# Gates and convolution inputs of a hybrid layer as seven-product blocks ahead of the attention, the convolution's projection behind it

## The chip, the cores and the metric

The kernel runs on one core of one Trainium2 chip. The metric is the device time of one execution in microseconds (us); the median of three runs before the change is 2365.08 us (2362.23 to 2366.52). One execution was taken with the hardware profiler: it took 2368.07 us, of which 2366.3 us lie between its first and last instruction. PE is the matmul engine (TensorE), ACT is ScalarE, DVE is VectorE, POOL is GpSimd, SP is the engine that issues most of the DMAs (SyncE).

## The reference, cut to what matters

One layer, sequence 1024, width 1024, all in fp32. The change is in the mixer between two feed-forward parts:

```python
h = modulate(rms_norm(x, g_mix[l]), sh2, sc2)
b_g, c_g, u, q, k, v, z_conv, z_attn = jnp.split(h @ w_in[l], IN_OFFSETS, axis=-1)
y_conv = (b_g * short_conv(c_g * u, conv_w[l])) @ w_conv_proj[l]
y_attn = sliding_window_attention(rope(q), rope(k), v, sinks[l]) @ w_attn_proj[l]
merged = sigmoid(z_conv) * y_conv + sigmoid(z_attn) * y_attn
x = x + gt2[:, None, :] * (merged @ w_out[l])
```

`short_conv` is a causal convolution of three taps in each channel. The attention has 16 heads in 4 groups and a window of 128. The feed-forward parts (inner width 2816) stand before and behind it.

## The kernel before

**Numbers.** Activations are held transposed, 8 tiles (`db` or `k`, 0 to 7) of 128 channels, in two halves `h` of 512 positions. A fp32 value is carried as two fp32r parts, hi and lo; a product of a 128x128 weight block and a 128x512 activation tile is three matmuls (`mm3`, L138, L140, L142: hi by hi, hi by lo, lo by hi). `split` makes the parts: ACT casts the hi part (L106), DVE, or POOL where the code says so, subtracts it for the lo part (L107). Tiles for weight parts turn in a ring of 8 (`w`), raw weights from DRAM in a ring of 4 (`wr`, loaded by `load_st`, L114), activations with their parts in rings of 28 (`t`, 128x2x512) and 16 (`x`, 128x512), scratch tiles (`q`, `u`, `s`) in short rings, PSUM in 8 banks (`ps`).

**Seven products.** The feed-forward parts compute a 2x2 block product with seven multiplications in place of eight (`gu_seven`, L392): `all_seven` forms the seven combinations of the activations once (DVE, L179 to L183), `seven_weights` forms those of each block's weights (DVE, L154 to L163, and seven splits), `product` (L195) issues the matmuls, 7 x 4 x 3 = 84 of 128x512 for a block, and DVE joins the partial results (L426, L432, L435). A block gives two output tiles in both halves. The mixer before does not use this.

**The mixer.** The down projection of the first feed-forward part ends with `down_part` for the last hidden tiles, half 0 and then half 1; behind tile 4 of half 1 the normalised input of half 0 is formed (`mix_h`, L275, L279, L290). The attention follows, 36 steps over 32 units (group, 128 positions); in step s stand `stage_c` of unit s-2 (scores, L853), `stage_b` of unit s-1 (transposes of q and k by PE, L832), `stage_a` of unit s (q, k, v: 24 matmuls of 128x384, L797 to L799), up to two pieces of the attention's projection (`proj_piece`, L950; its weight from `wap`, split into `t` tiles), `stage_e` of unit s-4 (L919, L920) and `stage_d` of unit s-3 (L896). Between a and b of one unit lies the rotary chain: DVE L807, L810, L813, then POOL L817, L818. In steps 0 to 4 an early gate is added (`early_gate`: 24 matmuls of one tile of z_attn, half 0, its weight in `t` tiles), in steps 0 to 3 also the mean square and `mix_h` of half 1, in steps 32 to 35 the same gates for half 1.

**The convolution's stage.** Behind the attention come the three other gates of z_attn, then for each pair of channel tiles (`gi`) the three inputs B, C and u (`wbcu`, 48 matmuls each with both halves), the taps (DVE L1056), and the projection of that pair (`wcp`), whose partial sums are added up in SBUF by DVE (L1085); then the eight gates of z_conv and the merge. 31 steps of the conditioning vector's products (`some_ada`, L225, each with a 512 KB load) lie in this stage, on a row that is loaded again (`crow_again`). `w_out` follows.

**Order.** PE runs in the order of the program. The rows of DVE, ACT, POOL and SP are put in order by a scheduler before the launch; each engine then works strictly in that order.

Of the kernel before, what the change touches and what calls it, by code (L numbers as in the profile page):

```python
# [13 lines left out]
P = 128  # L14
D = 1024
# [20 lines left out]
def tile_macaron_layer(  # L36
# [303 lines left out]

    class Hidden:
# [12 lines left out]
        def keep(self, t, dst):  # L354
            hi = tile_x(F32R)
            nc.scalar.copy(hi, t)  # L356
            nc.vector.tensor_tensor(f32r(t), t, f32(hi), op=ALU.subtract)  # L357
            nc.sync.dma_start(dst[:, 0, :], f32(hi))
            nc.sync.dma_start(dst[:, 1, :], t)

        def put(self, j, h, t):
            if j >= 4 * NCH:
                self.keep(t, self.last[j - 4 * NCH][h])
                return
# [9 lines left out]
            for k in PRODS:  # L374
                self.keep(parts[k], self.seven[p][k])
# [16 lines left out]
    def gu_seven(wgu, js, hid, ts, extra=lambda: None):  # L392
# [4 lines left out]
        def prep(j):  # L397
            ra, rb = load_st(wgu[j, 0]), load_st(wgu[j, 1])
            return seven_weights(ra[:, :HALF], ra[:, HALF:], rb[:, :HALF], rb[:, HALF:])

        def tail(state):

            j, w, oa, sa0 = state
            product(oa, w["q4"], xs["q4"], c0s, False, True)
            nc.vector.scalar_tensor_tensor(
                out=(raw := tile_x()), in0=oa, scalar=-1.0, in1=sa0, op0=ALU.mult, op1=ALU.mult)
            hid.put(j, 0, raw)

        ahead = [prep(j) for j in js[:1]]
        before = None  # L410
        for n, j in enumerate(js):
            w = ahead.pop(0)
            if n + 1 < len(js):
                ahead.append(prep(js[n + 1]))
# [4 lines left out]
            if before:  # L419
                tail(before)  # L420
# [5 lines left out]
            nc.vector.tensor_tensor(r1, r1, ob, op=ALU.add)  # L426
            nc.scalar.activation(r1, r1, AF.Silu)
# [7 lines left out]
            nc.vector.tensor_tensor(r5, r5, oa, op=ALU.add)  # L435
            nc.vector.scalar_tensor_tensor(
                out=(raw := tile_x()), in0=r5, scalar=-1.0, in1=r2, op0=ALU.mult, op1=ALU.mult)
            hid.put(j, 1, raw)
            extra()
            before = (j, w, oa, r1)  # L440
        tail(before)
# [151 lines left out]
    with tc.tile_pool(name="f1", bufs=2) as tmp:  # L593
# [143 lines left out]
        some_ada(6)  # L737
        gu_seven(w1gu, range(3, NJ), hid, ts, lambda: some_ada(1))
# [33 lines left out]
        hh, hl = hh2, hl2  # L772


    yat = by_half(tile_x)
# [516 lines left out]
```

## Time and profile before

| what | value |
|---|---|
| median of 3 runs | 2365.08 us |
| profiled execution | 2368.07 us, span 2366.3 us, mean granted PE clock 0.981 |
| PE busy | 2270.1 us (96%) |
| DVE busy | 1574.8 us (67%) |
| ACT busy | 1019.4 us (43%) |
| POOL busy | 395.0 us (17%) |
| read from DRAM, written | 256.19 MB, 91.49 MB |

PE is the engine to read first: its busy share is 96%, so time is lost only where PE waits or where its granted clock is below 1. The views used below are the page, groups of instructions by line (busy time, mean of one, idle time ahead and what ended it), waits, and busy time in chosen stretches. In the rows `ps<-t,w` means output from inputs; a row of the stretches gives for each engine busy time and, in brackets, the instructions.

### The profile page before, as it was taken

The page shows a single profiled execution, that of the slowest core. Times are in us where ns is not written, and L with a number is a line of the kernel's source. Part 1 is how long each engine was busy: PE and PEld are TensorE (multiplying, and loading weights), DVE is VectorE, ACT ScalarE, POOL GpSimd, SP SyncE. Part 2 cuts the span into 40 slices and gives each one's busy share as a digit, 9 for nine tenths or more (in the row PEclk, how much of TensorE's full clock was granted, in tenths as well). Part 3 has the DMA queues.
Part 4 walks back from the last instruction along what each step waited for, and adds up shares of the span by engine and source line. Part 5 has one row for each costly group of instructions (what it writes and reads, how often), then busy time and mean ns, then how long its engine had stood idle before and what let it go on. Part 6 is the DMA issues. An engine that isn't in the chain of part 4 may idle for free.

```text
span 2366.3 us, 30044 instructions
## 1 busy us (share of the span) xinstructions
PE 2270.1 (96%) x10608; PEld 1898.0 (80%) x10608; DVE 1574.8 (67%) x2796; ACT 1019.4 (43%) x2009; POOL 395.0 (17%) x461
## 2 busy tenths in 40 slices
PE   5899999999987899998999999999999999999997
PEld 4688888888876799996788888888888888888786
DVE  8888777858864567775543544444687776676875
ACT  4544444544443566554223121123554444454342
POOL 3000000006561334442000000001100000002644
PEclk9899999999998999998999999999999999999998
DMA  8165446799531201212422332115324553389922
GB/s 312 62 223 204 144 142 213 254 406 296 168 133 40 70 20 60 64 30 81 165 94 88 103 98 63 54 45 196 107 64 159 178 177 126 116 319 335 330 101 72
DMA packets 131767, 349.65 MB, mean 148 GB/s; under 512 B 18720, under 2 KB 20896, under 8 KB 131616
## 3 DMA queue, kind: packets, MB, share of 16 engines
q1 hardware_dynamic: 127008, 339.34, 40.9%
q0 software_dynamic: 4608, 8.39, 2.0%
q8 instruction: 83, 1.36, 0.2%
q14 instruction: 68, 0.56, 0.1%
HBM read 256.19 MB, written 91.49 MB: 147 GB/s over the span
## 4 chain that ended last, share of the span: by engine, by line
PE 86%; DVE 8%; DMA 2%; ACT 2%; issue 1%; POOL 0%; SPq 0%; DVEq 0%; ACTq 0%; POOLq 0%
PE ps L195 43%; PE ps L142 12%; PE ps L140 11%; PE ps L138 11%; PE ps L799 2%; PE ps L797 2%; PE ps L798 2%; DVE w L107 1%; PE ps L853 1%; DVE x L530 1%; PE ps L896 1%; DVE t L225 1%; DMA wr<-in_w2d_dram 1%; DVE u L275 1%; DMA x<-in_x_dram 1%
## 5 line engine op out<-in xcount | busy, mean ns | idle before, releaser
L195 PE MATMUL ps<-t,w 128*128 128x512 f32 x4956 | 1126.9, 390 | 5.5 <-DVE x L530 2.8
L195 PEld LDWEIGHTS ps<-t,w 128*128 128x128 f32 x4956 | 931.0, 188 | 201.0 <-DVE r L435 3.9
L106 ACT CAST w<-wr 128x512 fp32r<-128x512 f32 (+1 forms) x410 | 249.5, 612 | 637.5 <-PE ps L195 298.7
L107 DVE TENSOR_TENSOR w<-wr,w 128x512 fp32r<-128x512 f32 (+1 forms) x394 | 296.1, 756 | 213.3 <-ACT w L106 212.0
L140 PE MATMUL ps<-t,w 128*128 128x512 f32 (+1 forms) x1024 | 341.7, 388 | 4.7 <-DVE t L290 4.7
L476 POOL TENSOR_TENSOR x<-x,g 128x512 f32<-128x512 f32 x96 | 145.1, 1525 | 1061.5 <-DVE x L530 588.8
L138 PE MATMUL ps<-t,w 128*128 128x512 f32 (+1 forms) x896 | 292.7, 389 | 7.1 <-ACT t L279 7.1
L142 PE MATMUL ps<-t,w 128*128 128x512 f32 (+1 forms) x896 | 291.1, 387 | 0.0
L140 PEld LDWEIGHTS ps<-t,w 128*128 128x128 f32 x1024 | 193.8, 189 | 45.4 <-DVE t L290 6.9
L138 PEld LDWEIGHTS ps<-t,w 128*128 128x128 f32 x896 | 169.9, 190 | 43.2 <-ACT t L279 9.7
L142 PEld LDWEIGHTS ps<-t,w 128*128 128x128 f32 x896 | 169.7, 189 | 33.7
L106 ACT CAST w<-ws 128x512 fp32r<-128x512 f32 x177 | 109.7, 620 | 183.2 <-PE ps L195 137.7
L107 DVE TENSOR_TENSOR w<-ws,w 128x512 fp32r<-128x512 f32 x177 | 123.6, 704 | 31.5 <-ACT w L106 31.2
L138 PE MATMUL ps<-t,t 128*128 128x512 f32 x240 | 103.3, 431 | 25.4 <-ACT t L106 22.4
L142 PE MATMUL ps<-t,t 128*128 128x512 f32 x240 | 102.3, 426 | 5.1 <-DVE t L107 5.0
L140 PE MATMUL ps<-t,t 128*128 128x512 f32 x240 | 101.5, 423 | 0.9 <-POOL t L931 0.9
L530 DVE SCALAR_TENSOR_TENSOR x<-ps,mods,x 128x512 f32<-128x512 f32 (+1 forms) x104 | 73.0, 708 | 31.2 <-PE ps L195 15.9
L357 DVE TENSOR_TENSOR x<-x,x 128x512 fp32r<-128x512 f32 x145 | 91.9, 690 | 1.5 <-ACT x L356 1.4
L799 PE MATMUL ps<-w,t 128*128 128x384 f32 x256 | 87.7, 343 | 4.5 <-DVE t L290 4.5
L319 POOL TENSOR_TENSOR s<-s,q 128x512 f32<-128x512 f32 (+1 forms) x48 | 55.0, 1146 | 217.7 <-ACT q L315 216.1
L797 PE MATMUL ps<-w,t 128*128 128x384 f32 x256 | 89.4, 349 | 0.0
L798 PE MATMUL ps<-w,t 128*128 128x384 f32 x256 | 86.8, 339 | 0.0
(162 smaller groups left out, 2787.5 us busy)
## 6 DMA issues: line engine op xcount, KB each, us to landing
t<-hs SPq DMA_DIRECT2D x140, 512.0 KB, 9.9
hs<-x SPq DMA_DIRECT2D x277, 256.0 KB, 4.6
wr<-in_wada_dram SPq DMA_DIRECT2D x56, 512.0 KB, 3.7
wr<-in_w1gu_dram SPq DMA_DIRECT2D x44, 512.0 KB, 4.5
wr<-in_w2gu_dram SPq DMA_DIRECT2D x44, 512.0 KB, 3.6
wr<-in_wbcu_dram SPq DMA_DIRECT2D x24, 512.0 KB, 3.5
wr<-in_w1d_dram SPq DMA_DIRECT2D x22, 512.0 KB, 7.5
wr<-in_w2d_dram SPq DMA_DIRECT2D x22, 512.0 KB, 7.6
```

The lines of the kernel that those rows point to most:

```text
L106: nc.scalar.copy(hi, src)
L107: lo_engine.tensor_tensor(lo, src, f32(hi), op=ALU.subtract)
L138: mm(o, wh, xh, start=start, stop=False)
L140: mm(o, wh, xl, start=False, stop=False)
L142: mm(o, wl, xh, start=False, stop=stop)
L195: mm(o, a, b, start=first, stop=last, skip_group_check=True)
L357: nc.vector.tensor_tensor(f32r(t), t, f32(hi), op=ALU.subtract)
L476: nc.gpsimd.tensor_tensor(dst, dst, r, op=ALU.add)
L530: nc.vector.scalar_tensor_tensor(out=dst, in0=src, scalar=gate[:, db : db + 1], in1=dst if base is None else base, op0=ALU.mult, op1=ALU.add,)
L797: mm(o[:, :384], xh, wh, start=k == 0, stop=False)
L798: mm(o[:, :384], xh, wl, start=False, stop=False)
L799: mm(o[:, :384], xl, wh, start=False, stop=k == KT - 1)
```

## The change

All inputs of the mixer but q, k, v move ahead of the attention. Four gate tiles (tiles 0 and 1 of z_attn and z_conv) are plain products, 192 matmuls, written so that half 0 runs while half 1 is normalised; the mean square of half 1 stands at their k = 2, its `mix_h` at k = 4. Then `all_seven` forms the combinations and 18 blocks run as one stream: 6 pairs of gate tiles (`Gates`), 8 blocks of C and u (`Taps`, which form C times u and the convolution) and 4 of B (`Gated`, which multiply by the convolution). Sigmoids (32 tiles of 256 KB), the parts of the convolved input (`ycv`, 16 of 512 KB) and four combined tiles that are overwritten (`h12`) go to DRAM. The attention's steps carry no gates any more. The projection of the convolution (`conv_proj`, 24 matmuls with all eight input tiles summed in one bank) stands in the last attention steps and behind them; it reads `ycv` (`load_y`) and two gate tiles each. The same matmuls add up to: gates and convolution inputs 1920 before, 192 + 18 x 84 = 1704 now; the projection 384 in both. Loads of ACT's tables fall from 20 to 9, DMAs that SP issues rise from 882 to 986. The two feed-forward parts use the same code through classes; one `some_ada` step moves ahead of the first, 30 lie in the stream, up to three at a gate block and one at each other.

```diff
+    def seven_stream(blocks, ts, extra):
...
+            to.c21(oa)
...
+            to.c11(r1, ob)
...
+            to.c22(r5, oa)
+            extra(to)
+            before = (w, oa, to)
+        tail(*before)
...
+        some_ada(7)
+        gu_seven(w1gu, range(3, NJ), hid, ts, lambda to: some_ada(1))
...
+        def keep_gate(src, which, db, h, sign=1.0):
+            sg = tile_x()
+            nc.scalar.activation(sg, src, AF.Sigmoid, scale=sign)
+            nc.sync.dma_start(gates[which][db][h], sg)
+
+        class Gates(SevenOut):
+            def __init__(self, which, db):
+                self.at = (which, db)
+
+            def c11(self, r1, ob):
+                super().c11(r1, ob)
+                keep_gate(r1, *self.at, 0)
+
+            def c12(self, r2, oc):
+                super().c12(r2, oc)
+                keep_gate(r2, *self.at, 1)
+
+            def c22(self, r5, oa):
+                super().c22(r5, oa)
+                keep_gate(r5, self.at[0], self.at[1] + 1, 1, -1.0)
+
+            def c21(self, oa):
+                keep_gate(oa, self.at[0], self.at[1] + 1, 0, -1.0)
...
+                self.cu = [None, negative_product(r5, self.y12)]
+
+            def c21(self, oa):
+                self.cu[0] = negative_product(oa, self.y11)
...
+                for h in range(2):
+                    cu, t = self.cu[h], tile_x()
+                    nc.scalar.mul(t, cu, cw[2])
+                    for back in (1, 2):
+                        w = cw[2 - back]
+                        pieces = [(t[:, back:], cu[:, : HALF - back])]
+                        if h == 1:
+                            pieces.append((t[:, :back], self.cu[0][:, HALF - back :]))
+                        for dst, src in pieces:
+                            nc.vector.scalar_tensor_tensor(
+                                out=dst, in0=src, scalar=w, in1=dst, op0=ALU.mult, op1=ALU.add)
+                    convolved[self.i, h] = t
...
+            def done(self, i, h, b, sign=1.0):
+                t = convolved.pop((i, h))
+                if sign > 0:
+                    nc.vector.tensor_tensor(t, b, t, op=ALU.mult)
+                else:
+                    negative_product(b, t, t)
+                keep_parts(t, ycv[i][h])
...
+        plain = [(1, 0), (1, 1), (0, 0), (0, 1)]
+        wg = [load_w(wz[which, db]) for which, db in plain]
+
+        def some_gates(idx, h, between=lambda k: None):
+            banks = [bank() for _ in idx]
+            for k in range(KT):
+                between(k)
+                for i, o in zip(idx, banks):
+                    mm3([o], wg[i](k * P), [(hh[k][h], hl[k][h])], k == 0, k == KT - 1)
+            for i, o in zip(idx, banks):
+                keep_gate(o, *plain[i], h)
+
+        def between(k):
+            if k == 2:
+                rs[1] = stats[1].rstd()
+            if k == 4:
+                pb = spread(rs[1])
+                for d in range(KT):
+                    mix_h(pb, d, 1)
+
+        some_gates(range(4), 0, between)
+        ts = all_seven(tt, xT)
+        some_gates((0, 1), 1)
+        some_gates((2,), 1)
+        some_gates((3,), 1)
+
+        def gate_pair(which, db):
+            return wz[which, db], wz[which, db + 1], Gates(which, db)
+
+        def conv_pair(i):
+            return [(wbcu[k, 1], wbcu[k, 2], Taps(k)) for k in (i, i + 2)] + [
+                (wbcu[i, 0], wbcu[i + 2, 0], Gated(i, i + 2))]
+
+        seven_stream(
+            [gate_pair(1, 2), gate_pair(0, 2)] + conv_pair(0) + [gate_pair(1, 4)] + conv_pair(1)
+            + [gate_pair(0, 4)] + conv_pair(4) + [gate_pair(1, 6)] + conv_pair(5)
+            + [gate_pair(0, 6)],
+            ts, lambda to: some_ada(3 if isinstance(to, Gates) else 1),
+        )
...
+        for k in range(4):
+            t = tile_t()
+            nc.sync.dma_start(f32(t), h12[k])
+            hh[k][1], hl[k][1] = pair_of(t)
...
+        def load_y(h):
+            for i in range(KT):
+                t = tile_t()
+                nc.sync.dma_start(f32(t), ycv[i][h])
+                yparts[i, h] = pair_of(t)
+
+        def load_wc(dq):
+            wc[dq] = [load_w(wcp[g, dq]) for g in range(4)]
...
+        def conv_proj(db, h):
+
+            o = bank()
+            for i in range(KT):
+                c0 = (i % 2) * 512 + (db % 4) * P
+                mm3([o], wc[db // 4][i // 2](c0), [yparts[i, h]], i == 0, i == KT - 1)
+            sc, sa = stored_gate(0, db, h), stored_gate(1, db, h)
+            nc.vector.tensor_tensor(sc, sc, o, op=ALU.mult)
+            nc.vector.tensor_tensor(yat[db][h], yat[db][h], sa, op=ALU.mult)
+            nc.vector.tensor_tensor(sc, sc, yat[db][h], op=ALU.add)
             if h == 0:
+                ml[db] = tile_c(F32R)
+            mh[db][h] = tile_x(F32R)
+            split(mh[db][h], ml[db][:, h * HALF : (h + 1) * HALF], sc)
...
-            if s == 0:
-                rs[1] = stats[1].rstd()
-            if 1 <= s <= 3:
-                if s == 1:
-                    pb = spread(rs[1])
-                for d in ((0, 1, 2), (3, 4, 5), (6, 7))[s - 1]:
-                    mix_h(pb, d, 1)
-            if s >= len(units):
-                early_gate(s - len(units), 1)
+            if s == len(units):
+                load_wc(0)
+                load_y(0)
+                load_y(1)
...
-            if s < 5:
-                early_gate(s, 0)
-        early[4] = sigmoid(gate_tiles(1, 4, (1,))[0], "u")
+            if s > len(units):
+                conv_proj(s - len(units) - 1, 0)
+        conv_proj(3, 0)
+        for db in range(4):
+            conv_proj(db, 1)
+        load_wc(1)
+        for db in range(4, KT):
             for h in range(2):
-                nc.vector.tensor_tensor(yat[db][h], yat[db][h], sigmoid(o[h]), op=ALU.mult)
...
-        ycv = [tile_c(F32) for _ in range(KT)]
-        for gi in range(4):
-            ys = []
-            for i in (2 * gi, 2 * gi + 1):
...
-                for t in (1, 2, 0):
-                    w = load_w(wbcu[i, t])
...
-                        mm3(banks[t], w(k * P),
-                            [(hh[k][h], hl[k][h]) for h in range(2)], k == 0, k == KT - 1)
-                    some_ada(2 if t == 2 else 1)
...
-                        if gi == 0:
-                            nc.scalar.copy(dst, o[h])
-                        else:
-                            nc.vector.tensor_tensor(dst, dst, o[h], op=ALU.add)
...
+                conv_proj(db, h)
```

**PE, first steps of the attention.** Before, between the last matmuls of `stage_a` and the transposes of `stage_b` (L832) for the same unit stand the 24 matmuls of an early gate, of which the last three are shown; then `stage_a` of the next unit begins.

```order
L138 MATMUL ps_5991<-t_5838,t_5984 128x512
L140 MATMUL ps_5991<-t_5838,t_5984 128x512
L142 MATMUL ps_5991<-t_5838,t_5984 128x512
L832 MATMUL ps_6022<-ident,q_5960 128x128 x3
L797 MATMUL ps_6031<-w_5901,t_5803 128x384
L798 MATMUL ps_6031<-w_5901,t_5803 128x384
L799 MATMUL ps_6031<-w_5901,t_5803 128x384
```

Now the transposes (L1010) stand directly behind `stage_a` of the same unit (L975 to L977).

```order
L975 MATMUL ps_9069<-w_9064,t_5852 128x384
L976 MATMUL ps_9069<-w_9064,t_5852 128x384
L977 MATMUL ps_9069<-w_9064,t_5852 128x384
L1010 MATMUL ps_9109<-ident,q_9098 128x128 x3
L975 MATMUL ps_9118<-w_9039,t_5810 128x384
L976 MATMUL ps_9118<-w_9039,t_5810 128x384
L977 MATMUL ps_9118<-w_9039,t_5810 128x384
```

What stood between a unit's `stage_a` and its `stage_b` on PE has moved away.

**DVE, around the last feed-forward tiles.** Here `u` and `t` (L275, L290) are the normalised input of half 0. Before, the lo parts of the early gate's weight (L107, into `t` tiles) follow behind all eight, and the rotary chain of unit 0 (L807) is next.

```order
L290 SCALAR_TENSOR_TENSOR t_5823<-u_5824,mods,t_5823 128x512
L275 SCALAR_TENSOR_TENSOR u_5839<-x_3957,amod,ps_5798 128x512
L290 SCALAR_TENSOR_TENSOR t_5828<-u_5829,mods,t_5828 128x512
L290 SCALAR_TENSOR_TENSOR t_5833<-u_5834,mods,t_5833 128x512
L290 SCALAR_TENSOR_TENSOR t_5838<-u_5839,mods,t_5838 128x512
L107 TENSOR_TENSOR t_5983<-wr_5985,t_5983 128x512
L107 TENSOR_TENSOR t_5984<-wr_5985,t_5984 128x512
L807 TENSOR_TENSOR u_5958<-ps_5931,rope_5956 128x320
```

Now the lo parts of the fourth plain gate's weight go into the `w` ring, and stand among the same rows.

```order
L290 SCALAR_TENSOR_TENSOR t_5822<-u_5823,mods,t_5822 128x512
L290 SCALAR_TENSOR_TENSOR t_5828<-u_5829,mods,t_5828 128x512
L275 SCALAR_TENSOR_TENSOR u_5853<-x_3960,amod,ps_5805 128x512
L107 TENSOR_TENSOR w_5968<-wr_5966,w_5968 128x512
L290 SCALAR_TENSOR_TENSOR t_5834<-u_5835,mods,t_5834 128x512
L107 TENSOR_TENSOR w_5969<-wr_5966,w_5969 128x512
L290 SCALAR_TENSOR_TENSOR t_5840<-u_5841,mods,t_5840 128x512
L290 SCALAR_TENSOR_TENSOR t_5846<-u_5847,mods,t_5846 128x512
L290 SCALAR_TENSOR_TENSOR t_5852<-u_5853,mods,t_5852 128x512
```

The split of that weight has moved in among the L290 rows, ahead of four of them and behind the rest; the last of these rows belongs to k = 7.

**ACT, end of the attention.** The weight that is waited for is that of the attention's projection for the last group (`t` tiles from `wr`). Before, its two casts (third and fourth row) stand ahead of the four exponentials (L870) of unit 30.

```order
L106 CAST t_10199<-wr_10201 128x512
L106 CAST t_10200<-wr_10201 128x512
L106 CAST t_10234<-wr_10236 128x512
L106 CAST t_10235<-wr_10236 128x512
L106 CAST ws_10194<-ps_10190 128x256
L930 CAST t_9731<-s_10133 128x2x128
L870 ACTIVATE t_10170,den_10172<-t_10170,negm_10171 128x256 x4
L877 ACTIVATE es_10173<-es_10173 128x4
L106 CAST t_9270<-ps_10190 128x128
```

Now the cast of the same weight (last row, `t_13157`) stands behind the casts of the convolution's projection (`w`, of which the last is the first row), the copies, the exponentials (L1048) and the casts that follow them.

```order
L106 CAST w_13120<-wr_13117 128x512
L999 CAST vt_12999<-ps_12964 128x2x64
L1104 COPY s_13027<-ps_13018 64x256
L106 CAST t_13034<-ps_13036 128x512
L106 CAST t_13034<-ps_13043 128x512
L106 CAST ws_13088<-ps_13084 128x256
L1104 COPY s_13027<-ps_13018 64x256
L1048 ACTIVATE t_13064,den_13066<-t_13064,negm_13065 128x256 x4
L106 CAST t_12164<-ps_13084 128x128
L1108 CAST t_12625<-s_13027 128x2x128
L1055 ACTIVATE es_13067<-es_13067 128x4
L106 CAST t_13157<-wr_13159 128x512
```

The projection's weight has moved behind the exponentials of unit 30, on which it does not depend.

More of the change, by code (lines that the diff above doesn't have):

```diff
@@ L339, in swiglu_raw, with keep_parts @@
         return dst
+    def keep_parts(t, dst):
+        hi = tile_x(F32R)
+        nc.scalar.copy(hi, t)
+        nc.vector.tensor_tensor(f32r(t), t, f32(hi), op=ALU.subtract)
+        nc.sync.dma_start(dst[:, 0, :], f32(hi))
+        nc.sync.dma_start(dst[:, 1, :], t)
     class Hidden:
@@ L352, in __init__ @@
                          for _ in range(2)]
[L354 to L359, printed above, removed]
         def put(self, j, h, t):
             if j >= 4 * NCH:
-                self.keep(t, self.last[j - 4 * NCH][h])
+                keep_parts(t, self.last[j - 4 * NCH][h])
                 return
@@ L374, in put @@
             for k in PRODS:
-                self.keep(parts[k], self.seven[p][k])
+                keep_parts(parts[k], self.seven[p][k])
     def gu_mm(outs, w, hh, hl, halves):
@@ L399, in prep, with tail @@
             return seven_weights(ra[:, :HALF], ra[:, HALF:], rb[:, :HALF], rb[:, HALF:])
-        def tail(state):
-            j, w, oa, sa0 = state
+        def tail(w, oa, to):
             product(oa, w["q4"], xs["q4"], c0s, False, True)
[L405 to L409, printed above, removed]
+            to.c21(oa)
+        ahead = [prep(blocks[0])]
@@ L410, in gu_seven @@
         before = None
-        for n, j in enumerate(js):
+        for n, (_, _, to) in enumerate(blocks):
             w = ahead.pop(0)
-            if n + 1 < len(js):
-                ahead.append(prep(js[n + 1]))
+            if n + 1 < len(blocks):
+                ahead.append(prep(blocks[n + 1]))
             oa, oc = bank(), bank()
@@ L431, in gu_seven @@
             product(oc, w["q3"], xs["q3"], c0s, False, True)
-            nc.vector.tensor_tensor(r2, r2, oc, op=ALU.add)
-            nc.scalar.activation(r2, r2, AF.Silu)
+            to.c12(r2, oc)
             product(oa, w["q7"], xs["q7"], c0s, False, True)
[L435 to L441, printed above, removed]
+            to.c22(r5, oa)
+            extra(to)
+            before = (w, oa, to)
+        tail(*before)
+    def gu_seven(wgu, js, hid, ts, extra=lambda to: None):
+        seven_stream([(wgu[j, 0], wgu[j, 1], GateValue(hid, j)) for j in js], ts, extra)
     def down_seven(wd, hid, gate, ngate, xs, residual, extra=lambda: None):
@@ L775, in tile_macaron_layer @@
+        assert not steps
+        for k in range(4):
+            t = tile_t()
+            nc.sync.dma_start(f32(t), h12[k])
+            hh[k][1], hl[k][1] = pair_of(t)
     yat = by_half(tile_x)
```

171 lines of the change are left out of this document (71 added, 100 removed).

## The prediction

> **What bounds the kernel now.** I read the page first, then the busy time in stretches, then PE's waits, then the mean of one instruction by line.
>
> ```profile
> PE 2270.1 (96%) x10608; PEld 1898.0 (80%) x10608; DVE 1574.8 (67%) x2796; ACT 1019.4 (43%) x2009; POOL 395.0 (17%) x461
> ...
> L195 PE MATMUL ps<-t,w 128*128 128x512 f32 x4956 | 1126.9, 390 | 5.5 <-DVE x L530 2.8
> ```
>
> PE is busy in 96% of the span and DVE in 67%, so PE sets the time wherever it neither waits nor runs at a reduced clock. Where in the mixer does it do that? The stretches are the end of the down projection, the attention's start, its middle, its tail, the gates behind it, and the convolution's stage up to `w_out`. Columns: width, then busy time of PE, PEld, DVE, ACT and POOL, the granted PE clock, DMA share, GB/s.
>
> ```profile
> 672.22:698.40 26.18, 23.62 (x112) 19.54 (x111) 16.29 (x25) 13.80 (x23) 18.30 (x16) 1.00 0.49 171
> 698.40:803.00 104.60, 82.12 (x389) 67.79 (x387) 50.63 (x130) 45.69 (x103) 20.74 (x33) 0.82 0.15 49
> 803.00:1062.00 259.00, 256.81 (x1680) 235.51 (x1681) 191.73 (x610) 159.98 (x501) 110.81 (x196) 0.99 0.16 50
> 1062.00:1131.00 69.00, 57.18 (x263) 45.07 (x262) 36.12 (x72) 35.89 (x78) 13.63 (x18) 0.90 0.30 100
> 1131.00:1140.00 9.00, 9.00 (x41) 7.46 (x40) 7.91 (x13) 2.81 (x3) 0.00 (x0) 1.00 0.92 325
> 1140.00:1608.00 468.00, 468.00 (x2066) 387.66 (x2065) 210.78 (x332) 106.56 (x183) 2.17 (x15) 1.00 0.25 80
> ```
>
> Loss is width less PE's busy time, plus width times the missing part of the clock. The start loses 104.6 - 82.1 = 22.5 idle and 0.18 x 104.6 = 18.8 by the clock, **41.3**. The middle loses 2.2 + 2.6 = **4.8**, the tail 11.8 + 6.9 = **18.7**, together **64.8 us**. The convolution's stage loses nothing: 468.00 busy in 468.00 at clock 1.00. There only fewer matmuls help.
>
> ```profile
> PE ps L138 <- ACT t L106: 22.4, 8, 4.4
> PE ps L142 <- DVE t L107: 5.0, 6, 2.2
> PE ps L799 <- DVE t L290: 4.5, 5, 1.9
> PE ps L269 <- DVE nr L260: 2.6, 1, 2.6
> ```
>
> Columns: what waits and for what, us in total, times, longest. The 22.4 us are eight waits for weights of the early gates and of the attention's projection, whose casts stand behind other work on ACT.
>
> ```profile
> 724.00:728.00 4.00, 1.46 (x12) 1.27 (x10) 3.32 (x8) 1.94 (x4) 1.10 (x2) 1.00 0.06 12
> 728.00:732.00 4.00, 2.35 (x6) 1.63 (x7) 2.93 (x5) 1.39 (x3) 0.00 (x0) 0.72 0.05 7
> 732.00:736.00 4.00, 4.00 (x11) 3.13 (x10) 0.00 (x0) 0.00 (x0) 0.00 (x0) 0.50 0.31 93
> ```
>
> Behind one such wait: PE is idle most of 724 to 728, and the clock is 0.72 and then 0.50 in the next two stretches. A gap of about 4 us thus costs up to 4 x 0.28 + 4 x 0.50 = 3.1 us more.
>
> **The matmuls.** Gates and inputs fall from 1920 to 192 + 18 x 84 = 1704 matmuls of 128x512, 216 fewer.
>
> ```profile
> 672.22 0.39 PE L138 MATMUL ps<-t,w 128*128 128x512 f32 x1
> ...
> 688.09 0.39 PE L140 MATMUL ps<-t,w 128*128 128x512 f32 x1
> ```
>
> The listed 0.39 us is a pipelined length. Between these two rows lie 70 steps at full clock: 15.87 / 70 = 0.2267 us from start to start. So 216 x 0.2267 = **49.0 us** less; a block of 84 is 19.04 us of PE. The projection's 384 matmuls only move.
>
> **The stream of blocks.** Does DVE keep up with 19.04 us a block? Its durations:
>
> ```profile
> L107 DVE TENSOR_TENSOR w<-wr,w 128x512 fp32r<-128x512 f32 (+1 forms) x394 | 296.1, 756 | 213.3 <-ACT w L106 212.0
> L107 DVE TENSOR_TENSOR w<-ws,w 128x512 fp32r<-128x512 f32 x177 | 123.6, 704 | 31.5 <-ACT w L106 31.2
> L435 DVE TENSOR_TENSOR r<-r,ps 128x512 f32<-128x512 f32 x39 | 26.8, 687 | 21.4 <-PE ps L195 21.4
> L357 DVE TENSOR_TENSOR x<-x,x 128x512 fp32r<-128x512 f32 x145 | 91.9, 690 | 1.5 <-ACT x L356 1.4
> L1056 DVE SCALAR_TENSOR_TENSOR q<-ws,v,q 128x512 f32<-128x512 f32 x32 | 24.0, 750 | 1.9 <-ACT q L1054 1.8
> L225 DVE CUSTOM_DVE_ANT_0 wr<-wr,crow_again,v 128x1024 f32<-128x1024 f32 x31 | 39.8, 1285 | 63.9 <-DMA wr<-in_wada_dram 60.0 <-ACT crow_again L1028 3.9
> L275 DVE SCALAR_TENSOR_TENSOR u<-t,amod,ps 128x512 f32<-128x512 f32 x16 | 10.8, 742 | 3.9 <-PE ps L269 3.9
> L290 DVE SCALAR_TENSOR_TENSOR t<-u,mods,t 128x512 fp32r<-128x512 f32 x48 | 40.6, 873 | 1.1 <-ACT t L279 0.8
> L181 DVE SCALAR_TENSOR_TENSOR x<-x,x 128x512 f32<-128x512 f32 x28 | 19.3, 690 | 0.0
> L107 DVE TENSOR_TENSOR t<-x,t 128x512 fp32r<-128x512 f32 x32 | 20.8, 695 | 0.0
> ```
>
> A block's weights take four sums at 0.69 and seven lo parts, 4 x 0.756 + 3 x 0.704, together 7.9 us; the three joins 3 x 0.687 = 2.1. `Gates` add three conditioning steps of 1.285 (some 1.37 with the read of the sum): 14.1 in all. `Taps` add two products (1.4), four taps at 0.75, two pieces of one and two columns (some 0.4) and one conditioning step: 16.2. `Gated` add four products and four lo parts at 0.69 (5.5) and one such step: 16.9; but where the three steps of the gate block behind are put early into it, 19.6, 0.6 over PE. I take 1 us for each of the four, **+4**. Bounds: 0, and 14: the row L225 shows 60.0 us of waiting for such loads, some 2 for each of its 31, and seven of the stream's 30 such waits would reach PE in full. I cost stores (19 MB) and loads at nothing: with the blocks' and the conditioning weights some 53 MB in 343 us, 156 GB/s, beside 325 GB/s that the row 1131 to 1140 moved. Without that cover rival 3 holds.
>
> **The plain gates' start.** The normalisation of half 0 is as before; now 12 matmuls (2.7 us) stand at each k. The first lo part comes 2.7 late, about the 2.6 of row L269. The fourth weight's lo part stands among the L290 rows, four at 0.873 ahead: 3.2. The mean square 0.6, half clock 2: **+8.5** (3 to 12; the 4.5 of row L799, which is in the start's 41.3, goes).
>
> **DVE behind it.** From the spread of half 1 to the last join of the first block DVE has 8 x 0.742 + 8 x 0.873 (normalisation, 12.9), 16 combinations at 0.69 (11.0), 16 lo parts at 0.695 (11.1), 13 lo parts of weights (9.5), 8 sums (5.6), three conditioning steps (4.1) and three joins (2.1): 56.3 us. PE's work in that time: four k of four gates 10.9, half 1 of them 96 x 0.2267 = 21.8, one block 19.0, another product 2.7: 54.4. With the waits between rows **+5** (0 to 9).
>
> **The attention's start.** With the early gates their waits go; what is late next is the rotary chain, which their matmuls covered.
>
> ```profile
> L853 PE MATMUL ps<-t,ws 64*128 64x256 f32 (+1 forms) x384 | 30.9, 293 | 0.0
> L896 PE MATMUL ps<-ident,t 128*128 128x128 f32 x240 | 31.4, 273 | 0.0
> L807 DVE TENSOR_TENSOR u<-ps,rope 128x320 f32<-128x320 f32 x32 | 15.6, 489 | 8.4 <-PE ps L799 6.7 <-issue 1.6
> L813 DVE TENSOR_TENSOR q<-ps,rope 128x160 f32<-128x160 f32 x32 | 10.1, 315 | 0.0
> L817 POOL TENSOR_TENSOR q<-u,q 128x320 f32<-128x320 f32 x32 | 28.5, 891 | 65.6 <-DVE q L813 54.4 <-PE ps L142 6.6 <-DVE den L879 4.6
> L818 POOL COPY q<-q 128x64 f32<-128x64 f32 x32 | 8.6, 268 | 1.6
> ```
>
> DVE 0.489 + 2 x 0.315 and POOL 0.891 + 0.268 make 2.28, about 3.0 with the hand-overs. Unit 0 waits 3.0; PE's work of c (30.9 us in 32 units, 0.97 each), then also d (31.4 / 32 = 0.98) and e stand between in the next steps: 2.5, 2.1, 1.6, 0.6. That is 9.8, with 1.2 for the clock **+11** (6 to 16). The 2.6 us gap of row L269 lies in the first stretch, whose clock is 1.00; the 4 us gap halved the clock. The Trainium skill, "TensorE: Matmul & The Clock Gate", section "Part 1: The HAM clock gate (the "warmup" mystery)", says that the clock drops after an idle activity window of some 3.4 us, and both rows agree. By that rule none of these five gaps slows the clock and the time is 1.2 lower. By the row of the 4 us gap, if one of 3.0 counts, it is up to 1.9 higher.
>
> The middle keeps its steps: **+4.8**, as before.
>
> **The tail.** T is the end of the last `stage_a`, which frees the weight ring. Only then can the four weights of the convolution's projection be split: eight lo parts, 8 x 0.756 = 6.0. The raw buffer for the attention projection's weight comes free behind the first of them (its load then takes some 3.7), and its cast stands behind the exponentials of unit 30.
>
> ```profile
> L864 DVE CUSTOM_DVE_ANT_0 t<-ps,mask,nsink 128x256 f32<-128x256 f32 (+1 forms) x128 | 52.1, 463 | 30.8 <-PE ps L853 30.2
> L864 DVE DVE_READ_ACCUMULATOR2_ANT negm<- 128x1 f32 x128 | 10.6, 83 | 0.0
> L870 ACT ACTIVATE t<-t,negm 128x256 f32<-128x256 f32 (+1 forms) x128 | 62.0, 487 | 3.1 <-DVE negm L864 2.6
> L870 ACT ACTIVATION_READ_ACCUMULATOR t<-t,negm 128x1 f32 x128 | 24.0, 188 | 0.0
> L882 POOL TENSOR_SCALAR t<-t,den 128x256 f32<-128x256 f32 (+1 forms) x128 | 57.5, 468 | 96.8 <-DVE den L879 53.0 <-PE ps L896 16.6 <-ACT t L106 16.4
> L107 POOL TENSOR_TENSOR t<-wr,t 128x512 fp32r<-128x512 f32 x20 | 27.9, 1413 | 29.9 <-ACT t L106 25.9 <-PE ps L142 3.9
> wr<-in_wada_dram SPq DMA_DIRECT2D x56, 512.0 KB, 3.7
> ```
>
> On DVE behind T: 6.0, the rotary chain's 1.1, four maxima at 0.463 + 0.083: 2.2. On ACT then two more exponentials at 0.487 + 0.188 and small casts: about T + 14. PE is there at T + 3.4 (the chain and `stage_b`): **10.6** idle. POOL's lo part (1.413, behind 4 x 0.468) comes later still. The next two weights of this kind stand behind the eviction of a `conv_proj`, which waits for gate tiles that SP issues behind sixteen 512 KB loads: 4.5 each. Later ones some 2. Idle 21.6, and three long gaps with some 2.1 of clock loss each: **+28** (14, below the 18.7 of now, to 45, when the loads hold up four projections by 4 each). `w_out` begins behind a longer chain of the last tile: **+1.5** (0 to 3).
>
> **Sum.** Lost now 8.5 + 5 + 4 + 11 + 4.8 + 28 + 1.5 = 62.8, before 64.8. So -49.0 - 64.8 + 62.8 = **-51.0**. The profiled execution took 2368.07, 3.0 above the median of 2365.08; against it 2317, against the median **2314 us**. Fewer table loads on ACT (43% busy) and DVE's L1085 sums (PE solid there) count nothing.
>
> **Rivals.** (1) The ends are hidden better: stream and backlog cost nothing, the tail 18.7 as now: lost 44.5, saving 69, 2296; at all lower bounds (27.8 lost) 2279. For it: PE waits in L195 only 5.5 us in the whole span. Against: the order of ACT in the tail. Chance 0.25. (2) Losses grow: stream 14, tail 45, lost 89.8, saving 24, 2341. For it: the loads queued ahead of the gate tiles. Chance 0.2. (3) Slower: DVE, waiting for loads, becomes the bound of the stream. It decides from 51 / 18 = 2.8 us a block beyond my sum, some 22 us each; at 3.5 us the time is 2314 + 63 = 2377. Against it: three waits of 2 on top of the 14.1 of a gate block make 20, one on the others 18 to 19. Chance 0.04. (4) The change does not do what it says, since each block gives back its 49.0 / 18 = 2.7 us in waits: 2363. Chance 0.03.
>
> **How the numbers follow.** My forecast, 2314 with its own range 2300 to 2328, has 0.48. With rival 1 down to 2282 and rival 2 up to 2341, that range leaves out about 0.2. A measurement tells 0.2% (4.7 us) from no change: faster 0.93, same 0.03, slower 0.04.
>
> **What would show it.** `product`'s matmuls go from 4956 to 6468; starts lie 0.227 us apart in the stream, with DVE below 90% there; in the first attention steps PE waits 0.6 to 3 us for POOL's q and the clock stays near 1; in the tail one wait of some 10 us for the projection weight's cast and two of 4 to 5. Wrong: DVE near 100% through the stream, waits in most blocks, or a tail with a gap at each `conv_proj` for the gate tiles.

## The result

The changed kernel takes 2297.57 us (median of 4 runs, 2294.82 to 2300.95) against 2365.8 us of the kernel before (4 runs, 2362.23 to 2368.16): ratio 0.9714, 95% interval 0.9695 to 0.9732, some 68 us less. The forecast was 2314 us, 51 less, with a range of its own from 2300 to 2328; the time lies 2.4 us below that range, in the part that the forecast left to rival 1 (down to 2282).

The page after, engines and the group of `product`:

```profile
PE 2210.1 (96%) x10392; PEld 1849.1 (81%) x10392; DVE 1677.2 (73%) x2966; ACT 1060.4 (46%) x2095; POOL 394.4 (17%) x445
...
L195 PE MATMUL ps<-t,w 128*128 128x512 f32 x6468 | 1469.1, 389 | 4.8 <-DVE r L405 3.6
```

The matmuls of the seven products are 6468, 1512 more, and wait 4.8 us in all, most of it for a join by DVE; DVE's busy share has gone from 67% to 73%.

The stretches of the mixer, columns as before: the end of the down projection, the plain gates with the normalisation of half 1, the stream of 18 blocks, the first 80 us of the attention, its middle, its tail with the convolution's projection up to `w_out`.

```profile
671.31:697.50 26.19, 23.41 (x104) 18.87 (x103) 21.19 (x31) 13.64 (x22) 15.66 (x12) 0.94 0.48 171
697.50:754.05 56.55, 51.77 (x219) 41.94 (x218) 46.99 (x75) 37.43 (x66) 5.01 (x3) 0.94 0.29 103
754.05:1099.03 344.98, 343.61 (x1513) 283.54 (x1512) 247.80 (x404) 136.96 (x236) 7.11 (x7) 1.00 0.48 151
1099.03:1179.03 80.00, 72.14 (x497) 66.50 (x495) 49.55 (x177) 45.76 (x147) 32.86 (x60) 1.00 0.16 47
1179.03:1389.03 210.00, 209.69 (x1372) 192.44 (x1371) 156.45 (x496) 127.84 (x403) 89.04 (x157) 1.00 0.16 49
1389.03:1540.80 151.77, 137.24 (x635) 112.09 (x633) 89.43 (x168) 45.32 (x105) 17.39 (x25) 0.93 0.51 178
```

By the same reckoning (width less PE's busy time, and width times the missing part of the clock) the plain gates lose 4.8 + 3.4 = 8.2 us, the stream 1.4, the attention's start 7.9, its middle 0.3, the tail 14.5 + 10.6 = 25.1: 42.9, where the kernel before lost 64.8. The first stretch lost 2.6 before and now 2.8 + 1.6 = 4.4. With the matmuls that makes -49.0 - 21.9 + 1.8 = -69.1; the spans differ by 2366.3 - 2296.8 = 69.5.

PE's waits in the mixer, longest totals first (what waits and for what, us in total, times, longest):

```profile
PE ps L138 <- ACT t L106: 11.4, 3, 5.4
PE ps L1010 <- POOL q L995: 4.9, 4, 2.0
PE ps L142 <- POOL t L107: 2.5, 2, 2.4
PE ps L328 <- POOL s L319: 2.5, 1, 2.5
PE ps L269 <- DVE nr L260: 2.5, 1, 2.5
PE ps L142 <- DVE w L107: 2.0, 1, 2.0
PE ps L138 <- ACT t L1108: 1.5, 1, 1.5
PE ps L195 <- DVE r L405: 1.4, 2, 0.8
PE ps L1010 <- POOL q L996: 1.1, 1, 1.1
```

The eight waits of 22.4 us for casts have become three of 11.4, all in the tail; in their place at the attention's start stand the waits for the rotary chain, 4.9 + 1.1.

### The profile page after: what moved, and what is told of

The parts are those of the page before. It is cut to its first block, busy times and chain, and to the rows that moved or that the text cites. A ratio compares the mean times of both kernels' runs of the same rounds, so it can differ in the third digit from the quotient of the medians.

```text
span 2296.8 us, 30100 instructions
## 1 busy us (share of the span) xinstructions
PE 2210.1 (96%) x10392; PEld 1849.1 (81%) x10392; DVE 1677.2 (73%) x2966; ACT 1060.4 (46%) x2095; POOL 394.4 (17%) x445
## 4 chain that ended last, share of the span: by engine, by line
PE 87%; DVE 7%; issue 2%; DMA 2%; ACT 2%; POOL 1%; SPq 0%; DVEq 0%; POOLq 0%; ACTq 0%
PE ps L195 60%; PE ps L142 6%; PE ps L138 6%; PE ps L140 6%; PE ps L977 2%; PE ps L975 2%; PE ps L976 2%; DVE w L107 1%; PE ps L1031 1%; PE ps L1074 1%; DVE t L225 1%; DMA wr<-in_w2d_dram 1%; DMA wr<-in_wada_dram 1%; PE ps L1010 1%; PE ps L1098 1%
## 5 line engine op out<-in xcount | busy, mean ns | idle before, releaser
L195 PE MATMUL ps<-t,w 128*128 128x512 f32 x6468 | 1469.1, 389 | 4.8 <-DVE r L405 3.6
L107 DVE TENSOR_TENSOR w<-wr,w 128x512 fp32r<-128x512 f32 (+1 forms) x404 | 304.6, 760 | 137.8 <-ACT w L106 136.3
L106 ACT CAST w<-ws 128x512 fp32r<-128x512 f32 x231 | 143.5, 621 | 251.7 <-PE ps L195 202.1
L140 PE MATMUL ps<-t,w 128*128 128x512 f32 (+1 forms) x528 | 206.9, 392 | 4.9 <-DVE t L290 4.9
L107 DVE TENSOR_TENSOR w<-ws,w 128x512 fp32r<-128x512 f32 x231 | 161.7, 703 | 39.4 <-ACT w L106 38.9
L138 PE MATMUL ps<-t,w 128*128 128x512 f32 (+1 forms) x400 | 158.4, 396 | 6.3 <-ACT t L279 6.2
L142 PE MATMUL ps<-t,w 128*128 128x512 f32 (+1 forms) x400 | 155.9, 390 | 2.0 <-DVE w L107 2.0
L344 DVE TENSOR_TENSOR x<-x,x 128x512 fp32r<-128x512 f32 x161 | 102.7, 685 | 2.9 <-ACT x L343 2.7
L343 ACT CAST x<-x 128x512 fp32r<-128x512 f32 x161 | 88.7, 621 | 19.4 <-DVE x L431 12.1
L225 DVE CUSTOM_DVE_ANT_0 wr<-wr,crow_act,v 128x1024 f32<-128x1024 f32 x56 | 71.7, 1282 | 35.1 <-DMA wr<-in_wada_dram 35.0
L107 POOL TENSOR_TENSOR w<-wr,w 128x512 fp32r<-128x512 f32 (+1 forms) x16 | 21.5, 1355 | 401.5 <-ACT w L106 401.5
L569 DVE SCALAR_TENSOR_TENSOR x<-ps,mods,x 128x512 f32<-128x512 f32 (+1 forms) x104 | 72.6, 707 | 23.9 <-PE ps L195 12.5
L975 PE MATMUL ps<-w,t 128*128 128x384 f32 x256 | 88.3, 345 | 0.0
L977 PE MATMUL ps<-w,t 128*128 128x384 f32 x256 | 85.7, 335 | 0.0
```

Source lines behind the costliest of these rows:

```text
L106: nc.scalar.copy(hi, src)
L107: lo_engine.tensor_tensor(lo, src, f32(hi), op=ALU.subtract)
L138: mm(o, wh, xh, start=start, stop=False)
L140: mm(o, wh, xl, start=False, stop=False)
L142: mm(o, wl, xh, start=False, stop=stop)
L195: mm(o, a, b, start=first, stop=last, skip_group_check=True)
```

## Experiments

Each edits the changed kernel. "Changed" below is its second measurement, e1; times are medians, ratios to the kernel before with their 95% intervals.

### e1: the changed kernel again

> The changed kernel once more, as the reference for the next three on the same chip. Every theory: 2297 us, within 4, ratio to the kernel before 0.971.

2297.23 us, 0.9708 (0.9695 to 0.9721), as expected.

### e5: as many matmuls as before

```diff
             product(oc, w["q5"], xs["q5"], c0s, True, True)
+            if twice:
+                product(oc, w["q5"], xs["q5"], c0s, True, True)
```

> In each of the mixer's 18 blocks the 12 matmuls of product q5 are issued twice (the second start overwrites the first), so 216 matmuls come back, as many as the change took out. Theory (PE sets the stream's time and a matmul costs its start-to-start time of 0.2267 us): 49 us slower than the changed kernel, 1 or 2 less where waits are covered. Rival (the listed 0.39 us): 84 us. Rival (the stream waits on DVE and loads in part): 10 to 35 us.

2346.28 us, 0.9918 (0.9896 to 0.994): 49.0 over the changed kernel. The stretch of the stream:

```profile
751.19:1144.34 393.15, 392.31 (x1729) 324.17 (x1728) 249.13 (x404) 138.38 (x236) 7.10 (x7) 1.00 0.41 132
```

It took 344.98 in the changed kernel's first trace and 344.10 in e1's, and takes 393.15, with 216 matmuls more and no more waiting: against e1's trace 0.227 us each. The start-to-start time is the price; the listed 0.39 us (84 in all) is refuted, and so is a stream that waits in part.

### e6 and e7: how much room DVE has in the stream

```diff
         split(like(src, hi), like(src, lo), src, lo_engine)
+        for _ in range(again):
+            nc.vector.tensor_tensor(like(src, lo), src, f32(like(src, hi)), op=ALU.subtract)
```

> DVE computes the seven lo parts of each block's weights twice, 7 more rows of 128x512 in each of 18 blocks. Theory (a DVE row costs its start-to-start time, 0.60 us, so a block takes DVE 13.2 + 4.2 = 17.4 us of PE's 19.04): 0 to 6 us slower. Rival (a row costs its listed 0.69, a block 15.3 + 4.8 = 20.1): 19 us slower.

> The seven lo parts three times, 14 more rows a block. Theory (0.60 a row, 13.2 + 8.4 = 21.6 us a block, 2.6 over PE): 46 us slower, DVE near fully busy in the stream. Rival (0.69 a row, 15.3 + 9.7 = 25.0): 107 us slower. If the loads for the conditioning steps hold DVE up as well, some 20 more on either.

e6: 2305.55 us, 0.9745 (0.9726 to 0.9763), 8.3 over the changed kernel, a little more than the 0 to 6 of the theory. e7: 2354.9 us, 0.9951 (0.9934 to 0.9968), 57.7 over, where the theory had 46. The stream in e6, then in e7:

```profile
753.82:1103.19 349.37, 345.10 (x1513) 283.16 (x1512) 319.13 (x530) 138.04 (x239) 9.43 (x7) 1.00 0.46 150
```

```profile
754.26:1154.91 400.65, 360.70 (x1513) 289.58 (x1512) 390.52 (x656) 135.39 (x239) 9.55 (x7) 0.96 0.40 131
```

Read DVE's column: 247.80 in the changed kernel, 319.13 with 126 rows more, 390.52 with 252, 0.57 us a row. In e6 DVE is 91% busy, and against e1's trace the stream is 5.3 longer and begins 1.2 later; some 1.7 more are a clock of 0.62 behind a short wait at the attention's start, which e1's trace does not have (last section). In e7 DVE is 97% busy, and the stream takes 22.3 us a block (400.65 / 18). Rows at 0.60 on top of 13.2 would give 21.6, at the listed 0.69 on top of 15.3 it would be 25.0 and e6 19 us slower. The listed price is refuted by both. e7's stream is 11.9 us over 18 x 21.6; DVE is idle for 10.1 of it, of which it waits 5.6 for PE and 1.6 for a cast. The loads for the conditioning steps, which were to add 20, add nothing: its row L227, which reads them, has 0.1 us of idle time ahead of it in the whole stream.

Why a row costs less than its length is seen in DVE's timeline of the changed kernel (start, length):

```profile
746.01 0.68 DVE L183 SCALAR_TENSOR_TENSOR x<-x,x 128x512 f32<-128x512 f32 x1
746.61 0.69 DVE L161 TENSOR_TENSOR ws<-ws,wr 128x512 f32<-128x512 f32 x1
747.21 0.68 DVE L107 TENSOR_TENSOR t<-x,t 128x512 fp32r<-128x512 f32 x1
```

Each is listed with 0.68 to 0.69 and the next starts 0.60 after it.

### e2: stage a ahead of stage b

```diff
-            if at_(1):
-                stage_b(*at_(1))
             if at_(0):
...
                 stage_a(g, n)
+            if at_(1):
+                stage_b(*at_(1))
```

> Stage a of unit s stands ahead of stage b of unit s-1, so 4.3 us of matmuls lie between a unit's a and its b. Theory (the rotary chain, about 3 us, is what PE waits for in the first attention steps): the waits for POOL's q, 6.0 us in the changed kernel, fall below 1 us and the time falls by 5 to 6 us. Rival (the steps wait for something behind the chain, the casts of b or the rows of DVE, and the wait moves to stage c): the time stays within 2 us.

2308.34 us, 0.9752 (0.9738 to 0.9765): 11.1 slower than the changed kernel; neither number held. PE's waits in the first 80 us of the attention, and that stretch:

```profile
PE ps L1031 <- ACT t L106: 6.8, 5, 2.8
PE ps L1031 <- DVE t L107: 1.5, 2, 1.2
```

```profile
1097.46:1177.46 80.00, 71.68 (x447) 66.79 (x446) 46.59 (x164) 42.00 (x134) 30.47 (x54) 0.91 0.15 46
```

The waits for POOL's q are gone, as both held, and waits of stage c (L1031) for the casts of b stand in their place, 8.3 for 6.0. The clock falls to 0.91 with them, which neither had reckoned with: the start loses 8.3 idle and 7.2 by the clock, 15.5 where e1's trace loses 7.8. So the rotary chain is what the start waits for, but b's casts are a second chain with no cover once b moves.

### e10: a whole stage between a and b, and between b and c

```diff
-            if at_(2):
-                stage_c(*at_(2))
-            if at_(1):
-                stage_b(*at_(1))
+            if at_(3):
+                stage_c(*at_(3))
+            if at_(2):
+                stage_b(*at_(2))
...
-            if s > len(units):
-                conv_proj(s - len(units) - 1, 0)
+            if s > len(units) + 1:
+                conv_proj(s - len(units) - 2, 0)
```

> Stages b, c, d and e each stand one step later (b of unit s-2, c of s-3, e of s-5, d of s-4), 37 steps, and the first conv_proj one step later. A whole stage a then lies between a unit's a and its b, and another between its b and c. Theory (the start's waits are the rotary chain, and with a ahead of b alone they moved to c because b's casts had no cover): 5 to 6 us faster than the changed kernel. Rival (the extra step at the end, with little work in it, gives the gain back): within 2 us.

2285.97 us, 0.9666 (0.9653 to 0.968): 11.3 faster, twice what was expected. The start has no wait for the chain left; the rest of the gain lies in the tail, where the three waits for the projection's weight casts fell from 11.6 to 8.0 and POOL's from 2.4 to 1.2. Why they did was not followed further; of the chain alone the gain is some 6.7 us, the loss of the first 80 us falling from 7.83 in e1's trace to 1.17.

### e3, e4, e9: the tail

e3 writes the loads of `load_wc` and `load_y` behind stages e and d of step 32; e4 writes `load_y(1)` behind `conv_proj(3, 0)`.

```diff
         conv_proj(3, 0)
+        load_y(1)
         for db in range(4):
```

> In step 32 the loads of the convolution's projection weights and of its inputs are written behind the attention projection's pieces and stages e and d. Theory (the cast of the attention projection's weight stands behind the casts of the convolution's weights on ACT, and behind unit 30's exponentials): the first tail waits, 5.4 for the cast and 2.4 for POOL's lo part with some 3 us of slow clock, go, and the time falls by 7 to 11 us. Rival (what is late then is the convolution's projection, whose weights and inputs now come later, by about as much): within 3 us, with a new wait in front of the first conv_proj.

> The loads of half 1 of the convolution's parts (8 of 16) are written behind the projection's half 0, so gate tiles are issued ahead of them. Theory (the waits of 3.3 and 2.7 us in steps 34 to 36 come from evictions that wait for gate tiles behind sixteen loads): they shrink by 4 us or more and the time falls by 4 to 8 us. Rival (those casts wait in ACT's order for the eviction of conv_proj as such, not for its gate tiles): within 2 us, or slower by up to 4 where half 1 then arrives late.

e3: 2301.86 us, 0.9725 (0.9711 to 0.9738), 4.6 slower. e4: 2301.62 us, 0.9724 (0.9711 to 0.9738), 4.4 slower. Both theories fell. The longest tail waits of e3, then of e4:

```profile
PE ps L138 <- ACT t L106: 13.0, 2, 10.2
PE ps L138 <- ACT t L1108: 4.8, 1, 4.8
```

```profile
PE ps L138 <- ACT t L1108: 5.8, 1, 5.8
PE ps L138 <- ACT t L106: 5.4, 2, 2.7
PE ps L138 <- DMA t<-ycv: 3.3, 8, 0.8
```

In e3 PE still waits 4.8 in the first place, now for the attention's own output (L1108), and the wait for the next weight of the projection has grown to 10.2. ACT casts that weight behind the eviction of the first `conv_proj` (its sum leaving PSUM through DVE and the split), and DVE's first row of that eviction waits for a gate tile:

```profile
1431.97 0.69 DVE L1155 TENSOR_TENSOR q<-q,ps 128x512 f32<-128x512 f32 x1 [7.74 <-DMA q<-gate]
```

SP issues the gate tiles of this `conv_proj` behind the sixteen loads of `ycv`, at 1422.29 in e3 and at 1417.32 in the first trace of the changed kernel; moving those loads back made the gate tiles late. In e4, where they are issued ahead of eight of the loads, the two later waits are 2.7 each (3.3 and 2.7 without the edit), and half 1's parts now arrive late (DMA, 3.3). So gate tiles do not set the size of these waits in the changed kernel. Its first trace shows what does. DVE, behind `conv_proj`:

```profile
1428.37 0.69 DVE L1155 TENSOR_TENSOR q<-q,ps 128x512 f32<-128x512 f32 x1 [3.37 <-PE ps L142]
1428.97 0.69 DVE L1156 TENSOR_TENSOR x<-x,q 128x512 f32<-128x512 f32 x1
1429.69 0.69 DVE L1157 TENSOR_TENSOR q<-q,x 128x512 f32<-128x512 f32 x1
```

ACT right behind it, `x<-q` being the split of the merged tile and `t<-wr` the weight's casts:

```profile
1430.42 0.62 ACT L106 CAST x<-q 128x512 fp32r<-128x512 f32 x1 [4.99 <-DVE q L1157]
1430.94 1.13 ACT L106 CAST t<-wr 128x512 fp32r<-128x512 f32 x2
```

DVE waited 3.37 us for PE's last matmul of `conv_proj`; then come three rows, one cast, and only then the weight's cast, for which PE starts at 1431.61, 3.28 late. The weight, issued at 1414.82, took 11.3 us to land and had been there for 4.8 us. Its cast stands behind an eviction in ACT's order. The gate tile was close: issued at 1417.32, it took 10.8 us to land, 0.2 ahead of the matmul's end at 1428.33. In e1, the same program, it came last:

```profile
1426.20 0.69 DVE L1155 TENSOR_TENSOR q<-q,ps 128x512 f32<-128x512 f32 x1 [3.56 <-DMA q<-gate]
```

There PE waits 3.46. By the end of the last matmul, an earlier gate tile would win some 0.2 us of it; the rest is the eviction and its place in the order.

e9 takes the casts out of the tail: the last group's two weights are split in step 30 and kept for both halves.

```diff
+            if g == NKV - 1:
+                wapt[0] = last_wap[db // 4]
...
+            if s == len(units) - 2:
+                for q in range(2):
+                    last_wap[q] = load_w(wap[NKV - 1, q], tiles=[tile_t(), tile_t()])
```

> The attention projection's two weights of the last group are loaded and split in step 30, into t tiles of their own, and kept for both halves; in the tail no cast or lo part of them is left. Theory (the three tail waits, 5.4, 3.5 and 2.7 us, and POOL's 2.4 are all waits for these weights, of which the first stands behind the casts of the convolution's weights and the others behind the evictions of conv_proj): they go, with the slow clock behind them, 15 to 20 us faster than the changed kernel. Rival 1 (the wait moves on, as in the run with these loads ahead: the stages and conv_proj wait for the same casts): within 4 us. Rival 2 (16 loads of the convolution's parts now wait for t tiles and hold up conv_proj): slower, waits for DMA.

2284.71 us, 0.9652 (0.9637 to 0.9667): 12.5 faster. The longest waits left in its tail and just ahead of it:

```profile
PE ps L138 <- ACT t L1108: 4.8, 1, 4.8
PE ps L142 <- DVE t L107: 1.4, 1, 1.4
```

The three waits for casts are gone, and the theory held for them. Two are new: 4.8 in the first one's place (L1108, the cast of the attention's own output, behind the exponentials) and 1.4 for a lo part in the steps where the new splits are made. The sum fell short of 15 to 20 by about these.

### e8: the mean square later

```diff
-            if k == 2:
+            if k == 4:
                 rs[1] = stats[1].rstd()
-            if k == 4:
+            if k == 6:
                 pb = spread(rs[1])
```

> The mean square of half 1 stands at k = 4 of the plain gates and its spread at k = 6 (before 2 and 4). Theory (PE reaches the mean square 2.5 us before POOL's last square, and the gap is what halves the clock behind it): the 2.5 us wait goes, the slow clock of about 3 us with it, and DVE's backlog, which has room at 0.60 a row, takes the later start: 4 to 6 us faster than the changed kernel. Rival (half 1's normalisation comes later by what was won and its first gates wait for it): within 2 us.

2296.37 us, 0.9703 (0.9686 to 0.972), 0.9 below the changed kernel: no difference that these runs can tell. Its trace bears the theory out as far as the attention's start: PE no longer waits for half 1's mean square (2.5 in the first trace, 0.9 in e1), the clock behind it stays at 1.00, and the attention starts at 1093.98 us, against 1095.80 to 1099.03 in the eight traces whose programs are unchanged up to there (the first, e1 to e4 and e9 to e11). Then the wait of 1.98 us at the attention's start, which leaves the clock at 1.00 in the first trace and in e1, is followed by 0.53, which takes 1.7 us back. Whether the other three runs of e8 pay there too, no trace shows; inconclusive.

### e11: both edits that helped

> The edits of the last two together. If both theories hold, 20 to 26 us faster than the changed kernel, about 2273; if only the weights' holds, some 2280; if neither, 2297 within 4.

2273.13 us, 0.9613 (0.9597 to 0.963): 24.1 faster than the changed kernel, 93 faster than the kernel before. That is the sum of the two gains, 11.3 and 12.5, within the noise. Its attention's start and tail:

```profile
1095.80:1175.80 80.00, 78.82 (x544) 74.73 (x543) 54.16 (x192) 49.57 (x159) 34.59 (x63) 1.00 0.16 47
1385.80:1514.00 128.20, 125.73 (x591) 104.39 (x590) 79.07 (x152) 35.31 (x85) 11.81 (x22) 0.98 0.53 184
```

The start loses 1.2 us where the changed kernel lost 7.9, the tail 2.5 + 2.6 = 5.1 where it lost 25.1.

## Why the prediction was right, and where its sizes were off

- **The matmuls** (-49.0): right within the noise; e5 puts them back and costs 49.0.
- **What the kernel before lost** (64.8) was right as a sum to be removed: the early gates' waits are gone. What stands in their place was put at 62.8 and is 42.9, which is where nearly all of the 17 us between 51 and 68 come from (the first stretch, not in the sum, takes 1.8 back). By term:
- **DVE behind the plain gates** (+5) and **the stream** (+4): nothing and 1.4. PE's listed 0.39 was replaced by its start-to-start time, but DVE's rows were priced at their listed 0.69. At 0.60 the 56.3 us of rows would be some 49, under PE's 54.4, and a block takes DVE 247.8 / 18 = 13.8 us on average, where the listed prices (14.1, 16.2 and 16.9 for 6, 8 and 4 blocks) make 15.7. The 19.6 for a `Gated` block has three conditioning steps in all; with its own and three more it would have been 21.0. e6 and e7 show the price, and where DVE becomes the bound, rival 3's mechanism: at 319.13 / 18 = 17.7 us of rows a block PE still sets the time, at 21.7 DVE does.
- **The plain gates' start** (+8.5): 8.2 measured, by other parts. The first lo part was 0.3 late, not 2.7, the weight 2.0 and not 3.2 (four rows at 0.873 make 3.5, too); the mean square 2.5 in this trace, not 0.6; the clock took 3.4, not 2. That the sums agree is luck.
- **The attention's start and middle** (+11 and +4.8, together 15.8): 7.9 and 0.3; the first projection pieces' wait of 1.5 and 0.3 now lies within the first 80 us. The chain is there, with 6.0 for the 9.8 predicted: four waits 0.9 to 1.3 us shorter than I took and a last one of 1.1 for 0.6. None slowed the clock in this trace, so the 1.2 for it and the 2.6 of slow clock kept for the middle were not needed.
- **The tail** (+28): 25.1, but 14.5 idle and 10.6 by the clock, where I had 21.6 and 6.4. The first wait, 5.4 and 2.4, is the one named: the last cast stands behind unit 30's exponentials, as ACT's timeline shows.

```profile
1396.52 1.66 ACT L106 CAST w<-wr 128x512 fp32r<-128x512 f32 x3
...
1405.02 0.18 ACT L1048 ACTIVATION_READ_ACCUMULATOR t<-t,negm 128x1 f32 x1
1405.11 0.24 ACT L106 CAST t<-ps 128x128 fp32r<-128x128 f32 x1
1405.26 0.40 ACT L1108 CAST t<-s 128x256 fp32r<-128x256 f32 x1
1405.56 0.20 ACT L1055 ACTIVATE es<-es 128x4 f32<-128x4 f32 x1
1405.67 1.12 ACT L106 CAST t<-wr 128x512 fp32r<-128x512 f32 x2
```

The cast that PE waits for starts at 1405.67, behind the last exponential and three short rows. The size, 10.6, was off at both ends, and not on DVE. T, the end of the last `stage_a`, is 1394.91, and DVE's last maximum ends at 1404.25, T + 9.3, as the terms 6.0, 1.1 and 2.2 said:

```profile
1404.18 0.07 DVE L1042 DVE_READ_ACCUMULATOR2_ANT negm<- 128x1 f32 x1
```

```profile
1394.58 0.33 PE L977 MATMUL ps<-w,t 128*128 128x384 f32 x1
...
1406.33 0.79 PE L138 MATMUL ps<-t,t 128*128 128x512 f32 x1 [5.43 <-ACT t L106]
```

From there to PE's start it took 2.1 us, not the 4.7 up to T + 14; and PE was there at T + 6.0, not T + 3.4, since 12 matmuls of the attention's projection and stages e, d and c stand between `stage_a` and `stage_b`. Each end is 2.6 us off. The exponentials themselves set this wait: e3 and e9, where the weight's cast is out of the way, still wait 4.8 there for L1108 behind them.

For the next two waits the step failed in its cause. They were put down to gate tiles behind sixteen loads, 4.5 each; they are 3.3 and 2.7, and e4 and ACT's timeline show that an eviction ahead in ACT's order makes all but some tenths of that. The mechanism that was named shows at its full size in e3, where the edit makes the gate tiles late.

- **`w_out`** (+1.5): a wait of 0.3.

Rival 1, the ends hidden better, with 2296 us, came nearest to the time, and for its reason in the backlog and the stream. Its tail of 18.7 did not come; that its number is met to 2 us all the same is luck, since the attention's start and middle lost 7.6 less than it had.

## What to carry to other kernels

Price every engine's rows by the distance between starts in a stretch without waits, DVE's as well as PE's: the listed length was 15% too long for DVE, and that made the fullest blocks of a stream look bound in which DVE had a quarter of its time free. When a wait stands in a tail, look up which row is ahead of the awaited one in its own engine's order before blaming a load, and then what that row waits for: two edits of loads made it worse, and taking the awaited work out of the stretch altogether removed it. Moving one stage past another covers one chain and uncovers the next; moving it by a whole step covered both.

## What was not expected of the hardware

The same short gap slows the clock in one execution and not in the next, and then the next gap pays. The 2.47 us wait for the reciprocal of the mean (L269) and the two stretches of 3.4 us behind it, in the first trace of the changed kernel and in e1, the same program; PE's clock is the third column from the right. The last two rows of e1 are the stretches behind its next gap, 1.86 us in front of the first lo part:

```profile
690.65:693.12 2.47, 0.00 (x1) 0.00 (x1) 2.34 (x7) 0.89 (x2) 1.92 (x2) 1.00 0.11 23
693.12:696.52 3.40, 3.40 (x14) 2.85 (x15) 2.13 (x4) 1.34 (x3) 1.27 (x1) 0.66 0.61 214
696.52:699.92 3.40, 3.40 (x14) 2.66 (x12) 3.40 (x6) 3.40 (x6) 0.00 (x0) 0.83 0.00 0
```

```profile
690.87:693.34 2.47, 0.00 (x2) 0.00 (x1) 2.35 (x7) 0.90 (x2) 1.92 (x2) 1.00 0.28 32
693.34:696.74 3.40, 3.40 (x19) 2.98 (x20) 2.12 (x4) 1.34 (x3) 1.27 (x1) 1.00 0.58 208
696.74:700.14 3.40, 2.09 (x10) 1.40 (x8) 3.40 (x6) 3.40 (x6) 0.00 (x0) 1.00 0.00 0
700.69:704.09 3.40, 3.40 (x10) 2.33 (x10) 3.40 (x6) 3.40 (x7) 0.00 (x0) 0.69 0.60 225
704.09:707.49 3.40, 2.38 (x6) 1.82 (x6) 3.40 (x5) 3.40 (x7) 1.70 (x1) 0.50 0.08 15
```

In the first the clock is 0.66 and 0.83 behind the gap of 2.47; in the other it is 1.00 there, and 0.69 and 0.50 behind the shorter one. Over 690 to 724 us, width times the missing clock is 5.1 us in both traces, so the slow clock came later and was not saved. In the tail of the changed kernel a gap of 2.73 us halved the clock, too (0.51 and 0.50 in the 6.8 us behind it). At the attention's start one of 1.98 us did not in five traces (the first, e1, e4, e5, e9) and did in four (e3 0.67, e6 and e7 0.62, e8 0.53, each in the 3.4 us behind it). The rule that the prediction weighed, the Trainium skill, "TensorE: Matmul & The Clock Gate", section "Part 1: The HAM clock gate (the "warmup" mystery)", that an idle window of some 3.4 us has to pass, is not borne out by these gaps, which are shorter. The free-running window that the same section describes would fit that the outcome changes between executions; no run here shows the window itself. The trace of the kernel before held a row against the rule, too, beside the two that the prediction read: from 702.59 us its clock is 0.50, behind waits of only 1.21 and 0.63 us.

For a sum, a single gap of about 2 us is to be priced at nothing or at 1.7 us, by chance (in e8, (0.47 + 0.03) x 3.4). A stretch with several such gaps is better priced as a whole: the start of the plain gates, 690 to 724, lost 3.4 or 5.1 us by the clock in each of the eleven traces of the changed kernel and its variants that leave its order there alone, whichever gap it was that paid.
